# A LoRA-adapted linear layer on one core: four 8 MB chunks in three buffers in place of eight 4 MB chunks in six, and a small early store cut into seven

## The chip, the cores and the metric

The kernel runs on one core of a Trainium2 chip. Its engines work side by side and wait for each other by semaphores: TensorE (PE; PEld is its loading of weights) multiplies, VectorE (DVE), ScalarE (ACT) and GpSimd (POOL) copy and cast, and SyncE (SP) issues the transfers, which sixteen DMA engines carry out between the chip's main memory (DRAM) and the core's own memory (SBUF, 128 partitions). TensorE writes into PSUM. The metric is the device time of one execution in microseconds; less is better.

## The reference

```python
x_flat = x.reshape(-1, in_dim)            # x: 16 x 2048 x 256, float32
y = x_flat @ W                            # W: 256 x 256
lora_out = x_flat @ lora_A                # 256 x 16
lora_out = lora_out * lora_E
lora_out = lora_out @ lora_B              # 16 x 256
y = y + scale * lora_out
```

The 32,768 rows of x are 33.5 MB, and the output is as large. The rest is small.

## The kernel before

The low-rank part is folded into the weights once: W_eff = W + A (E scale B) is made at the start (lines 213 to 223 on TensorE, 165 to 177 on VectorE) and kept in bf16. After that each row of x is multiplied by a 256 x 256 matrix.

The rows are cut into eight chunks (`N_CHUNKS`) of 4 MB. In a chunk each partition holds 32 consecutive rows (`ROWS`) of 1 KB, so one transfer of a chunk is 128 contiguous pieces of 32 KB, one a partition. A chunk is loaded into a buffer of its own, a "home"; there are six (`N_HOMES`), 192 KB a partition. The result of a chunk is written over its input in the same home and stored from there. Chunks 6 and 7 use the homes of chunks 0 and 1 again, and their loads wait for the stores of those (line 105). The first chunk is loaded in three pieces of 8, 8 and 16 rows a partition, so that work can begin sooner (`LOAD_PIECES`).

Inside, the work goes by groups of four rows a partition (`CG`), 64 groups in all. Each group passes four engines:

- GpSimd casts 128 x 1024 float32 values to bf16 into `stage` (line 151). At a piece's first group it waits for that piece's load (line 148).
- TensorE transposes the group (line 196), two bf16 values at a time as one float32 word; ScalarE copies the result from PSUM to `xt` (line 162).
- TensorE multiplies (line 204, eight matmuls), and VectorE copies the product from PSUM back to the home (line 181). After a chunk's last group it signals `s_chunk`; after the very first group it signals `s_first`.

`stage`, `xt` and the two PSUM tiles are double-buffered.

All transfers are issued by SyncE, in the order of the list `ORDER`, into one queue. The DMA engines work that queue off in order: a transfer that is issued early stands behind those issued before it. A store (`S0` to `S7`) is issued when its chunk is done (line 127). All of a chunk must be done, as it is stored by one transfer. The last entry of `ORDER` is issued after the block of the five programs (line 241).

One transfer is unusual: after the loads of chunk `EARLY_AFTER`, SyncE waits for the first group (line 124) and stores 16 partitions x 128 bytes of the first result (line 125). The full store S0 writes the same bytes again later, after a wait for that early store (line 129).

Of the kernel before, what the change touches and what calls it, by code (L numbers as in the profile page):

```python
# [10 lines left out]
ALU = mybir.AluOpType  # L11


ROWS = 32
N_CHUNKS = 8
N_HOMES = 6
LOAD_PIECES = {0: [8, 8, 16]}

ORDER = [
    "L0", "L1", "L2", "L3", "L4", "L5",  # L20
    "S0", "S1", "L6", "L7", "S2", "S3", "S4", "S5", "S6", "S7",
]

EARLY_AFTER = 1

CG = 4
GPC = ROWS // CG
N_GROUPS = N_CHUNKS * GPC

# [6 lines left out]
def kernel(  # L36
# [16 lines left out]
    KT = K // P  # L53
    assert N == N_CHUNKS * ROWS * P and K == M and KT == 2

    x_chunks = x_flat.rearrange("(c p b) k -> c p b k", p=P, b=ROWS)
    y_chunks = out_flat.rearrange("(c p b) m -> c p b m", p=P, b=ROWS)

    sbuf, psum, sem = nc.alloc_sbuf_tensor, nc.alloc_psum_tensor, tc.alloc_semaphore
    homes = [sbuf(f"home{h}", [P, ROWS, K], FP32) for h in range(N_HOMES)]  # L60
    stage = [sbuf(f"stage{i}", [P, CG, K], BF16) for i in range(NS)]
# [12 lines left out]
    pieces = []  # L74
    for c in range(N_CHUNKS):
        s = 0
        for n in LOAD_PIECES.get(c, [ROWS]):
            pieces.append((c, s, s + n))
            s += n
    loaded = {pc: sem(f"loaded_{pc[0]}_{pc[1]}") for pc in pieces}  # L80
    set_up_loaded = {n: sem(f"loaded_{n}") for n in ("w", "a", "b", "e")}
    stored_of = {c: sem(f"stored_{c}") for c in range(N_CHUNKS - N_HOMES)}
    stored_rest = sem("stored_rest")
# [10 lines left out]
    s_early = sem("early_stored")  # L94

    def home(c):
        return homes[c % N_HOMES]

    sync, gpsimd, scalar, vector, tensor = nc.sync, nc.gpsimd, nc.scalar, nc.vector, nc.tensor

    def sync_program():
        def load(pc):
            c, s, e = pc
            if c >= N_HOMES:
                sync.wait_ge(stored_of[c - N_HOMES], 16)
            sync.dma_start(out=home(c)[:, s:e, :], in_=x_chunks[c, :, s:e, :]).then_inc(loaded[pc], 16)

        load(pieces[0])
        for name, to, of in (
            ("w", w_sb, W.rearrange("(q t) m -> q t m", t=KT)),  # L110
            ("a", a_sb, lora_A.rearrange("(q t) r -> q t r", t=KT)),
            ("e", e_sb, lora_E[:, None]),
            ("b", b_sb, lora_B),
        ):
            sync.dma_start(out=to[:], in_=of).then_inc(set_up_loaded[name], 16)
        for step in ORDER[:-1]:
            c = int(step[1:])
            if step[0] == "L":
                for pc in pieces:
                    if pc[0] == c and pc != pieces[0]:  # L120
                        load(pc)
                if c == EARLY_AFTER:

                    sync.wait_ge(s_first, 1)
                    sync.dma_start(out=y_chunks[0, :16, 0, :32], in_=home(0)[:16, 0, :32]).then_inc(s_early, 16)
            else:
                sync.wait_ge(s_chunk, c + 1)
                if c == 0:
                    sync.wait_ge(s_early, 16)
                sync.dma_start(out=y_chunks[c], in_=home(c)[:]).then_inc(stored_of.get(c, stored_rest), 16)  # L130

    def gpsimd_program():
# [97 lines left out]
    with tc.tile_critical(no_gpsimd_drain=True):  # L230
        sync_program()
        gpsimd_program()
        scalar_program()
        vector_program()
        tensor_program()
# [3 lines left out]

    last = int(ORDER[-1][1:])  # L240
    nc.sync.dma_start(out=y_chunks[last], in_=home(last)[:])
# [35 lines left out]
```

## Time and profile before

| What | Value |
|---|---|
| Time, median of 9 runs | 164.93 us (164.56 to 165.23) |
| Time of the profiled execution | 164.85 us |
| Its span, from the first to the last instruction | 163.1 us (163.07) |
| Mean granted TensorE clock | 0.828 |
| Bytes moved, mean rate | 67.43 MB, 414 GB/s |
| TensorE matmuls busy | 99.6 us (61%) |
| VectorE busy, copies of line 181 | 79.5 us (49%), 64 of 1225 ns |
| GpSimd busy, casts of line 151 | 67.1 us (41%), 64 of 1040 ns |
| ScalarE busy, copies of line 162 | 66.1 us (41%), 64 of 1012 ns |
| Issue to landing of a 4 MB load, median | 20.0 us |
| Issue to landing of a 4 MB store, median | 42.0 us |

The last two rows contain the time that a transfer stands in the queue. In the slice rows of the page the span is cut into 40 equal parts, and each digit is a busy share in tenths (9 is 90% or more); PEclk is the TensorE clock that was granted. The view of one DMA queue gives its packets, their MB, and the time that they took as a share of sixteen engines' time; small packets of 4 bytes are the semaphore writes that end each transfer on each engine.

### The profile page before, as it was taken

To read this page: it belongs to the slowest core of one execution; us is meant where nothing else is said; L and a number is where in the kernel's file an instruction comes from. 1 tells how busy PE (TensorE), PEld (TensorE's weight loads), DVE (VectorE), ACT (ScalarE), POOL (GpSimd) and SP (SyncE) were. 2 spreads that over 40 slices of the span, in tenths; PEclk is the share of its full clock that TensorE was granted. 3 is DMA by queue.
4 is the path that set the end of the run, shared out by engine and by line. 5 is a ranking of instruction groups with operands and counts; after the bars stand their busy time and mean duration, and the time that the engine had idled before them with its cause. 6 is when DMAs were issued, how large, how long until landed. Compare 5 with 4: busy or idle time off the path is not lost. (4 is left out here: it accounts for less than half of the span.)

```text
span 163.1 us, 2148 instructions
## 1 busy us (share of the span) xinstructions
PE 99.6 (61%) x778; PEld 82.4 (51%) x778; DVE 79.5 (49%) x66; ACT 66.1 (41%) x65; POOL 67.1 (41%) x70
## 2 busy tenths in 40 slices
PE   0399948999999999999930099999960000000000
PEld 0268837888888888888820078888840000000000
DVE  0115862788888888888860025888880000000000
ACT  3043732777767676777720025677720000000000
POOL 1444615777777777777500155777500000000000
PEclk9999995999999999999996557999997555555555
DMA  4999998998998999899999999999999999999990
GB/s 163 420 450 454 394 507 386 434 466 386 490 410 386 506 394 388 386 434 460 402 434 450 410 466 410 420 458 410 418 466 410 450 434 418 466 402 426 458 402 16
DMA packets 2979, 67.43 MB, mean 414 GB/s; under 512 B 528, under 2 KB 544, under 8 KB 672
## 3 DMA queue, kind: packets, MB, share of 16 engines
q1 hardware_dynamic: 2976, 67.41, 96.9%
q14 instruction: 3, 0.02, 0.0%
HBM read 33.85 MB, written 33.56 MB: 413 GB/s over the span
## 5 line engine op out<-in xcount | busy, mean ns | idle before, releaser
L181 DVE COPY home<-psum_y 128x1024 f32<-128x1024 f32 x64 | 78.4, 1225 | 32.8 <-PE psum_y L204 29.9
L151 POOL CAST stage<-home 128x1024 bf16<-128x1024 f32 x64 | 66.4, 1040 | 48.8 <-PE psum_xt L196 24.9
L162 ACT COPY xt<-psum_xt 128x1024 bf16<-128x1024 bf16 x64 | 64.8, 1012 | 52.7 <-PE psum_xt L196 52.7
L204 PE MATMUL psum_y<-weff,xt 128*128 128x256 bf16 x512 | 70.3, 283 | 0.7
L204 PEld LDWEIGHTS psum_y<-weff,xt 128*128 128x128 bf16 x512 | 48.2, 101 | 14.9 <-issue 6.7
L196 PE MATMUL psum_xt<-ident,stage 128*128 128x128 f32 x260 | 42.6, 291 | 14.0 <-PEq L189 14.0
L196 PEld LDWEIGHTS psum_xt<-ident,stage 128*128 128x128 f32 x260 | 33.1, 151 | 16.1 <-issue 15.1
L216 PE MATMUL psum_y<-ident,a_sb 128*16 128x128 f32 x2 | 0.6, 397 | 6.7 <-DMA a_sb<-in_lora_A_dram 6.7
L167 DVE TENSOR_SCALAR ate<-psum_y,e_sb 16x256 f32<-16x256 f32 x1 | 0.5, 472 | 7.4 <-PE psum_y L216 7.4
L216 PEld LDWEIGHTS psum_y<-ident,a_sb 128*16 128x16 f32 x2 | 0.1, 88 | 6.7 <-issue 6.7
L222 PE MATMUL psum_y<-b_sb,ate 16*128 16x256 f32 x4 | 2.1, 670 | 0.0
L177 DVE TENSOR_TENSOR weff<-w_sb,psum_y 128x512 bf16<-128x512 f32 x1 | 0.7, 687 | 2.4 <-PE psum_y L222 2.4
L162 ACT ACT_TABLE_LOAD x1 | 1.3, 1283 | 0.9 <-SPq L230 0.9
L222 PEld LDWEIGHTS psum_y<-b_sb,ate 16*128 16x128 f32 x4 | 1.2, 320 | 0.5 <-issue 0.3
L133 POOL MEMSET ident<- 128x128 f32 x1 | 0.2, 204 | 0.5 <-SPq L230 0.5
L135 POOL TENSOR_SCALAR_AFFINE_SELECT ident<-ident 128x128 f32<-128x128 f32 x1 | 0.3, 292 | 0.2 <-POOL ident L133 0.2
L258 POOL MEMSET const-float32-0.0<- 128x1 f32 x1 | 0.1, 98 | 0.2 <-issue 0.2
L258 POOL MEMSET const-bfloat16-1.0<- 128x1 bf16 x1 | 0.1, 102 | 0.0
L258 POOL MEMSET const-uint8-127<- 128x1 uint8 x1 | 0.1, 102 | 0.0
L258 POOL MEMSET const-float32-1.0<- 128x1 f32 x1 | 0.1, 98 | 0.0
## 6 DMA issues: line engine op xcount, KB each, us to landing
out_dram<-home SPq DMA_DIRECT2D x8, 4096.0 KB, 42.0
home<-in_x_dram SPq DMA_DIRECT2D x7, 4096.0 KB, 20.0
home<-in_x_dram SPq DMA_DIRECT2D x2, 1024.0 KB, 5.2
home<-in_x_dram SPq DMA_DIRECT2D x1, 2048.0 KB, 10.1
w_sb<-in_W_dram SPq DMA_DIRECT2D x1, 256.0 KB, 5.0
a_sb<-in_lora_A_dram SPq DMA_DIRECT2D x1, 16.0 KB, 4.7
e_sb<-in_lora_E_dram SPq DMA_DIRECT2D x1, 0.1 KB, 4.5
b_sb<-in_lora_B_dram SPq DMA_DIRECT2D x1, 16.0 KB, 4.0
```

Of the source, the lines that this page charges most:

```text
L133: gpsimd.memset(ident[:], 0.0).then_inc(s_ident, 1)
L135: gpsimd.affine_select(out=ident[:], in_=ident[:], compare_op=ALU.not_equal, fill=1.0, base=0, pattern=[[-1, P]], channel_multiplier=1,).t ...
L151: gpsimd.tensor_copy(out=stage[g % NS][:], in_=home(c)[:, b:b + CG, :]).then_inc(s_stage, 1)
L162: scalar.copy(out=xt[g % NX][:], in_=halves).then_inc(s_xt, 1)
L167: vector.tensor_scalar(out=ate[:], in0=psum_y[0][:R, :KT, :P], scalar1=e_sb[:], scalar2=float(scale), op0=ALU.mult, op1=ALU.mult,).then_in ...
L177: vector.tensor_add(out=weff[:], in0=w_sb[:], in1=psum_y[1][:, :KT, :]).then_inc(s_free, NY)
L181: vector.tensor_copy(out=home(c)[:, b:b + CG, :], in_=psum_y[g % NY][:]).then_inc(s_free, 1)
L196: ins = tensor.transpose(psum_xt[i % NT][:, b, :], words[:, b, :], ident[:])
L204: ins = tensor.matmul(psum_y[i % NY][:, b, :], xt[i % NX][:, b, t, :], weff[:, t, :], start=(t == 0), stop=(t == KT - 1),)
L216: ins = tensor.transpose(psum_y[0][:R, t, :P], a_sb[:, t, :], ident[:])
L222: ins = tensor.matmul(psum_y[1][:, t, :], ate[:, t, :], b_sb[:], start=True, stop=True)
L258: nc = _bacc.Bacc("TRN2", target_bir_lowering=False, num_devices=1)
```

## The change

Eight chunks of 32 rows a partition become four of 64. A home is twice as large, and three take the place of six, so the memory used is the same. A chunk's transfer is 128 pieces of 64 KB. Chunk 0 is loaded in four pieces (8, 8, 16 and 32 rows), chunk 3 in two of 32; chunks 1 and 2 in one. The order keeps its kind: loads into all homes, two stores, the load that reuses a home, the remaining stores.

The early store is issued after the load of chunk 0 rather than of chunk 1 (in both cases 8 MB of loads stand ahead of it), and is seven transfers in place of one. They store 8, 4, 12, 14, 15, 2 and 1 partitions, 128 bytes each, from different places of the first group's four rows. S0 waits for all of them.

```diff
-ROWS = 32
-N_CHUNKS = 8
-N_HOMES = 6
-LOAD_PIECES = {0: [8, 8, 16]}
-
-ORDER = [
-    "L0", "L1", "L2", "L3", "L4", "L5",
-    "S0", "S1", "L6", "L7", "S2", "S3", "S4", "S5", "S6", "S7",
-]
-
-EARLY_AFTER = 1
+ROWS = 64
+N_CHUNKS = 4
+N_HOMES = 3
+LOAD_PIECES = {0: [8, 8, 16, 32], 3: [32, 32]}
+
+ORDER = ["L0", "L1", "L2", "S0", "S1", "L3", "S2", "S3"]
+
+EARLY_AFTER = 0
+EARLY_LINES = [8, 4, 12, 14, 15, 2, 1]
...
                     sync.wait_ge(s_first, 1)
-                    sync.dma_start(out=y_chunks[0, :16, 0, :32], in_=home(0)[:16, 0, :32]).then_inc(s_early, 16)
+                    for b, n in enumerate(EARLY_LINES):
+                        sync.dma_start(out=y_chunks[0, :n, b % CG, b // CG * 32:][:, :32], in_=home(0)[:n, b % CG, b // CG * 32:][:, :32]).then_inc(s_early, 16)
...
                 if c == 0:
-                    sync.wait_ge(s_early, 16)
+                    sync.wait_ge(s_early, 16 * len(EARLY_LINES))
```

## The prediction

> **What bounds the kernel now.** I read the page's DMA rows first. 67.4 MB go through one DMA queue, and the sixteen DMA engines are full from the first slice to the last but one; TensorE has gaps, and its clock falls in two of them.
>
> ```profile
> PEclk9999995999999999999996557999997555555555
> DMA  4999998998998999899999999999999999999990
> q1 hardware_dynamic: 2976, 67.41, 96.9%
> ```
>
> Next I read the DMA view of 124 to 158 us, where nothing computes and only stores run, and of 8.2 to 13 us, where 128 packets of 16 KB run.
>
> ```profile
> DMA packets 499, 14.78 MB, mean 435 GB/s; under 512 B 48, under 2 KB 48, under 8 KB 48
> q1 hardware_dynamic: 499, 14.78, 100.6%
> ...
> DMA packets 143, 2.09 MB, mean 435 GB/s; under 512 B 15, under 2 KB 15, under 8 KB 15
> q1 hardware_dynamic: 143, 2.09, 101.9%
> ```
>
> A packet is one partition's contiguous piece. In the first view 451 are of 32 KB: 1.006 x 16 x 34 us / 451 = 1.213 us each; in the second 1.019 x 16 x 4.8 / 128 = 0.611 us. The individual packet records give 1,209.5 and 607.4 ns from one start to the next on an engine, so 2 x 607.4 - 1209.5 = 5 ns of a packet are fixed and the rest is bytes. One 4 MB chunk is 8 packets an engine, 9.68 us with its completion. I call this a unit. The order before is 6 units of loads, 2 of stores (S0, S1), 2 of loads (L6, L7), 6 of stores.
>
> The tail shows that the engines don't end together. This is the DMA view of 158 to 163.1 us, 40 slices of 0.13 us:
>
> ```profile
> GB/s 0 771 1285 257 257 257 0 0 0 257 0 0 0 0 0 0 0 0 257 0 0 0 0 0 0 0 0 0 0 0 0 0 0 0 0 0 0 0 0 0
> ```
>
> Fifteen engines have started their last packet by 158.7 and end by 159.9; one starts packets at 159.2 and 160.4 and ends at 161.62. The span ends 1.45 us after that. By the packet records one engine takes 1,284 to 1,293 ns a packet from 63.5 to 82.7 and one again from 105 to 122.7, some 77 ns too many, while the others take 1,213. Those are the stores S0, S1 and S2, S3, during which compute runs; beside L6 and L7, and in S4 to S7 where compute has ended, none is slow. I read it as one engine that is slow where stores and compute overlap; that is inferred from four stretches.
>
> Last I read the timeline for compute, which is hidden under DMA and must only be early enough. These are GpSimd's first and last cast of the last two chunks, VectorE's last copies, and SyncE's issue of the last store (start, us, engine).
>
> ```profile
> 92.99 2.02 POOL L151 CAST stage<-home 128x1024 bf16<-128x1024 f32 x2 [12.69 <-DMA home<-in_x_dram]
> ...
> 115.81 1.04 POOL L151 CAST stage<-home 128x1024 bf16<-128x1024 f32 x1 [0.31 <-PE psum_xt L196]
> ...
> 119.62 2.58 DVE L181 COPY home<-psum_y 128x1024 f32<-128x1024 f32 x2 [0.24 <-PE psum_y L204]
> 122.59 0.33 SPq L241 DMA_DIRECT2D out_dram<-home  x1
> ```
>
> Sixteen groups (64 rows) take 122.20 - 92.99 = 29.2 us from the first cast, 0.53 us after L6's last packet ended at 92.46. S7, issued at 122.59, first moves bytes at 149.3: 27 us of slack.
>
> **The change, part by part.** *Descriptors.* Of L1, L2 and S0 to S3, 48 packets of 64 KB an engine replace 96 of 32 KB: 48 x 5 ns = 0.24 us less. Six completions fewer at 6 ns add 0.04. No row has a 64 KB packet or a 64 KB step between partitions. Nearest are 16 KB and 32 KB packets, both at 27 GB/s an engine, so by these 0.28 us is gained; if each is cut into two again, nothing. I take 0.2.
>
> *Early store.* Each 128-byte packet with its completion takes 22 ns in the records. If a DMA puts one line on an engine, the most is 7 x 22 = 0.15 us; all 56 lines on one engine would be 1.2; an engine with none saves 0.02. I take 0.1. The Trainium skill (DMA: Bandwidth & Descriptors, "Why a DMA increments its semaphore by 16 and not by 1") says that a DMA uses the largest number of engines up to 16 that divides its slowest dimensions, the lowest-numbered ones. By that engine 0 would get seven packets, engine 15 none, which makes the estimate a staircase of 0 to 0.15 us; the trace has 16 lines only, so no row shows it.
>
> On SyncE the wait for the first group's copy (to 14.34) now stands before L1 and L2. The same 8 MB are queued ahead, which last to 22.8, and seven issues at 0.35 to 0.47 us put L1 at 17.0 to 17.6. A load's first packet follows its issue by 1.0 to 1.45 us (0.94 to 1.96 and 2.40 in the opening), so 3.7 us of cover remain and this costs nothing. The wait ahead of S0 has until 62 us.
>
> *Coarser chunks in the middle.* Chunk 0 ends where chunk 1 did, at 40.6; the first 64-row load lands at 42.65 (unit 4) instead of 32-row ones at 32.9 and 42.65. TensorE waits some 3 us; with 29.2 us for the chunk it ends by 72.4, and S1 is needed at 81.5: 7.7 us of cover after issue and latency. Chunk 2 landed at 62.7 and ends at most 16 x 1.41 = 22.6 later, 95; S2's place in the queue comes at 120. L3 waits for S0, about 83, and is needed at 101. These cost nothing while the covers last. Where loads first give way to stores the DMA view of 59 to 62.5 us has 367 GB/s, some 0.5 us lost; the change keeps that place, and so, I take it, that loss.
>
> *The end, where the cover goes.* L3 is units 11 and 12, S2 units 13 and 14, S3 units 15 and 16. Before, the last loads were units 9 and 10 and six stores stood behind them. Now the last 64 rows must be computed between the landing of L3's first half and the end of S2, three units or 29 us, and S3 can't start on any row before all are done. Worked out:
>
> - L7 ended on its last engine at 102.53. Less 0.2 and plus 0.1 from above. The slow engine now also meets compute in the first half of S1 (to about 93, not 82.7): 8 packets x 77 ns = 0.6 more, bounds -1.1 (no lag at all) to 0.7. One more load unit, 9.68: L3's first half ends at 112.7, the first cast is at 113.2.
> - Sixteen groups: 29.2 from the row above; the second half is there at 122.9, before group 9 (11.5 us after the first cast) needs it, so they run through. The restart after 93 us is cold, as it was before.
>
> ```profile
> 25.03:28.45 3.42, 3.42 (x17) 2.81 (x17) 0.82 (x1) 1.01 (x1) 1.75 (x2) 0.50 1.07 460
> 86.47:100.12 13.65, 5.95 (x28) 4.97 (x29) 1.78 (x2) 2.02 (x2) 4.10 (x4) 0.50 1.01 435
> ```
>
> (Stretch, its length, busy time of PE, PEld, DVE, ACT and POOL, granted clock, DMA share, GB/s.) TensorE restarted at 24.90 and was at full clock at 28.45, 3.5 us; at 94.17 and full at 100.12, 5.95 us. Cold groups take 2.5 us, warm ones 1.41, so a cold stretch as short as the first saves 2.4 x (1 - 1.41/2.5) = 1.1 us. I take 28.9, with 28.1 to 29.2. The Trainium skill (TensorE: Matmul & The Clock Gate, "What's actually happening") has the window of 3.4 us run free of the kernel; by it the cold time could be 3.4 to 6.8 us and differ between runs, which would stretch my upper end by 0.4.
>
> - Last copy ends at 142.1; issue 0.39 later as before (122.20 to 122.59); first packet 1.0 to 1.45 later, I take 1.2: 143.7. S2 would have ended at 139.4 on the fifteen engines and near 143 on the slow one, so the queue is empty for up to 4 us.
> - S3's eight packets of 64 KB an engine are 8 x 2.414 = 19.3; first packets from a standing queue took 0.2 to 0.7 us too long in the opening (8 KB ones), I take 0.3, with 0 to 0.7: end 163.3, tail 1.45, span 164.75.
>
> Against its own span of 163.07 that is +1.7. The profiled execution took 164.85 us, 0.08 under the median, so the time is 164.93 + 1.7 = 166.6 us. The lag of the one engine is absorbed in the wait; only 0.3 us would have been gained had the queue stayed full.
>
> **Rivals.** *Last chunk late* (forecast, 166.6, own range 165.3 to 167.8): for it speaks that three units are 29.0 us and cast, compute, issue and latency are 0.53 + 28.9 + 0.39 + 1.2 = 31.0. Against it: by the slow engine, whose S2 takes 16 x 77 ns = 1.2 us longer, only 0.8 of the 2.0 is idle.
>
> *Faster, the lag goes.* If the uneven early lines or longer packets keep the slow engine from falling behind, L3's first half lands by 111.0, cast 111.5; with the short cold stretch 28.1, issue 0.39, latency 1.0 and no slow first packet, S3 starts at 141.0 and ends at 160.3: span 161.8, time 163.6. It decides from about 2 us off my sum, and needs both the lag and the cold time to shrink; the packet rows show the lag unchanged by an early store of one packet an engine.
>
> *No change.* Lag as before and the short cold stretch: the sum falls by 0.6 + 0.8 to 165.2, and with the short latency of 1.0 us to 165.0.
>
> *Slower by rate.* 64 KB pieces or pitch move fewer bytes: 48 x 2.41 = 116 us are exposed, 1% is 1.2 us, 167.8 with the gap. Against it: 16 and 32 KB run at one rate. *It doesn't do what it says*: packets stay at 32 KB; 166.8, as the gap comes from the order.
>
> **How the numbers follow.** About 0.2% is what a measurement of this kernel can tell from no change. Last chunk late 0.71 (packets cut again within it), rate 0.09, no change 0.07, lag gone 0.13. Slower: 0.80; same 0.07; faster 0.13. Range 164.8 to 167.8: it takes in the bounds of lag, cold time and latency, and leaves most of the faster case and the rate case out.
>
> **What would show it.** A gap of 1 to 4 us in the DMA slices near 140 to 144; the last issue of SyncE at about 142.5 rather than 122.6; GpSimd's wait for the last load ended at 113.2 (111.5 would be the lag gone); engines ending together instead of 2.6 us apart; 64 KB packets at 2.41 us. If the DMA row has no gap before the last store, the forecast is wrong in its main step.

## The result and the profile after

The changed kernel is slower: 165.45 us (median of 19 runs, 165.06 to 166.02) against 164.78 us for the kernel before in runs beside it (57 runs, 164.41 to 165.3). The ratio is 1.0042, with a 95% interval of 1.0034 to 1.0051, or +0.7 us where +1.7 was forecast. The profiled execution took 165.57 us, its span is 163.79 us; before it was 163.07. The time lies inside the range and on the side that was forecast; the difference came out 1 us smaller.

The same rows of the page, now of the changed kernel:

```profile
PEclk9999985799879999999999965555599999955555
DMA  5999999979969989699799899989999989659955
q1 hardware_dynamic: 2192, 67.41, 96.4%
```

Over the span the DMA engines are nearly as full as before (96.4% against 96.9%); the slices of 6 and 5 from 139.2 us on hold a gap. SyncE's issues from 70 us on (start, us, engine):

```profile
71.21 0.34 SPq L129 DMA_DIRECT2D out_dram<-home  x1
83.50 1.02 SPq L104 DMA_DIRECT2D home<-in_x_dram  x2
118.38 0.34 SPq L129 DMA_DIRECT2D out_dram<-home  x1
142.11 0.34 SPq L240 DMA_DIRECT2D out_dram<-home  x1
```

These are S1, L3's two halves, S2 and S3. The last store is issued at 142.11, near the forecast of 142.5, and by then the queue has run dry. The DMA view of 136 to 150 us in 40 slices of 0.35 us shows it:

```profile
DMA  0009994000040000000990000099000009900000
GB/s 0 0 0 562 1123 1123 187 0 0 0 0 187 0 0 0 0 0 0 0 1311 1685 0 0 0 0 0 1311 1685 0 0 0 0 0 1872 1123 0 0 0 0 0
```

The packets are in step, and their starts stand in bunches; the row counts a packet's bytes where it starts. By the packet records, fifteen engines started their last packet of S2 by 138.2 and ended between 139.60 and 140.6; one started its last at 140.16 and ended at 142.65. All sixteen start S3 at 142.95 to 143.10. So fifteen engines wait for 2.4 to 3.35 us, and one for 0.3. They also end together, within 0.15 us, where one engine trailed before. Here are 158 to 163.79 us in slices of 0.14 us:

```profile
GB/s 0 0 0 0 0 0 0 0 0 0 0 0 0 5886 1358 0 0 0 0 0 0 0 0 0 0 0 0 0 0 0 0 0 0 0 0 0 0 0 0 0
```

The compute between L3's first half and S3: GpSimd's first cast of the chunk and VectorE's last two copies.

```profile
113.06 2.02 POOL L150 CAST stage<-home 128x1024 bf16<-128x1024 f32 x2 [24.75 <-DMA home<-in_x_dram]
...
139.13 2.58 DVE L180 COPY home<-psum_y 128x1024 f32<-128x1024 f32 x2 [0.24 <-PE psum_y L203]
```

Sixteen groups take 139.13 + 2.58 - 113.06 = 28.65 us. TensorE's clock was low from 95.16 to 119.05 (the first two numbers are the stretch and its length, the 0.50 is the granted clock):

```profile
95.16:119.05 23.89, 4.80 (x23) 3.92 (x24) 1.22 (x1) 2.02 (x2) 4.10 (x4) 0.50 0.97 418
```

### The profile page after: what moved, and what is told of

Same layout as the page of the kernel before. It is cut to its first block, busy times and chain, and to the rows that moved or that the text cites. A ratio compares the mean times of both kernels' runs of the same rounds, so it can differ in the third digit from the quotient of the medians.

```text
span 163.8 us, 2142 instructions
## 1 busy us (share of the span) xinstructions
PE 100.7 (61%) x778; PEld 83.4 (51%) x778; DVE 79.5 (49%) x66; ACT 66.1 (40%) x65; POOL 67.0 (41%) x70
## 3 DMA queue, kind: packets, MB, share of 16 engines
q1 hardware_dynamic: 2192, 67.41, 96.4%
## 5 line engine op out<-in xcount | busy, mean ns | idle before, releaser
L180 DVE COPY home<-psum_y 128x1024 f32<-128x1024 f32 x64 | 78.4, 1224 | 52.4 <-PE psum_y L203 49.9
L203 PE MATMUL psum_y<-weff,xt 128*128 128x256 bf16 x512 | 71.2, 285 | 0.9
L203 PEld LDWEIGHTS psum_y<-weff,xt 128*128 128x128 bf16 x512 | 48.7, 102 | 15.1 <-issue 7.0
L195 PEld LDWEIGHTS psum_xt<-ident,stage 128*128 128x128 f32 x260 | 33.6, 153 | 34.6 <-issue 33.6
```

What stands on the lines that cost most here:

```text
L180: vector.tensor_copy(out=home(c)[:, b:b + CG, :], in_=psum_y[g % NY][:]).then_inc(s_free, 1)
L195: ins = tensor.transpose(psum_xt[i % NT][:, b, :], words[:, b, :], ident[:])
L203: ins = tensor.matmul(psum_y[i % NY][:, b, :], xt[i % NX][:, b, t, :], weff[:, t, :], start=(t == 0), stop=(t == KT - 1),)
```

## The experiments

Times are medians; each ratio is to the kernel before in runs on the same chip, with its 95% interval.

**E1, the last store in two halves.** It takes away what makes S3 wait for all 64 rows.

```diff
+            if g == N_GROUPS - GPC // 2 - 1:
+                vector.drain().then_inc(s_half, 1)
...
+                if step == ORDER[-1]:
+                    sync.wait_ge(s_half, 1)
+                    sync.dma_start(out=y_chunks[c, :, :32, :], in_=home(c)[:, :32, :]).then_inc(stored_rest, 16)
...
-    nc.sync.dma_start(out=y_chunks[last], in_=home(last)[:])
+    nc.sync.dma_start(out=y_chunks[last, :, 32:, :], in_=home(last)[:, 32:, :])
```

> The changed kernel with its last store in two halves; the first half (32 rows a partition) is issued as soon as its eight groups are done. Theory A (the queue runs empty before the last store, and behind that gap the one engine that is slow beside compute sets the next limit): no gap; that engine ends S2 at 142.65 and needs 16 packets of 1.21 us more, so it ends at 162.0 and the span is 163.3 to 163.5 (163.8 in the changed kernel), the time 165.0 to 165.2; the engines end some 3 us apart again. Theory B (the loss comes from larger packets or the seven early stores, not from the gap): the time stays at 165.4 to 165.5. Theory C (the gap is all of it, no engine lags behind it): the time falls to 164.5 or lower, as the packets alone save 0.2 to 0.3.

165.25 us, ratio 1.0025 (1.0013 to 1.0037). The half stores are issued at 130.88 and 142.50:

```profile
118.46 0.34 SPq L134 DMA_DIRECT2D out_dram<-home  x1
130.88 0.34 SPq L129 DMA_DIRECT2D out_dram<-home  x1
142.50 0.33 SPq L247 DMA_DIRECT2D out_dram<-home  x1
```

The gap is gone, and one engine trails again, which I call the trailing engine from here on. Its tail, 158 to 163.5 us in slices of 0.14 us:

```profile
GB/s 477 238 715 1907 238 0 238 0 0 0 0 0 238 0 0 0 0 0 0 0 0 238 0 0 0 0 0 0 0 0 0 0 0 0 0 0 0 0 0 0
```

Fifteen engines end between 159.25 and 160.1 and one at 162.14 (expected 162.0). Theory A holds for where the end comes from. By the medians and ratios the gap cost 0.2 to 0.3 us, not 0.7: without it the kernel is still 0.48 us slower than before. The size is rough: the intervals of the two ratios overlap, and the fastest run of the changed kernel (165.06) equals the fastest of E1 (165.07).

**E6, the same gap closed in another way**: `LOAD_PIECES` for chunk 3 is [8, 8, 16, 32] instead of [32, 32].

> The changed kernel with the load of the last chunk in pieces of 8, 8, 16 and 32 rows, so that its groups begin some 7 us earlier. Theory A: the groups of the last 32 rows start at 122.8 with TensorE warm, the last store is issued near 139.5, before the lagging engine is free; that engine (S2 to 142.7, then 19.3) sets the end, span 163.3 to 163.6, time 165.1 to 165.3, as with the store in two halves. If the lag did not matter: 164.5.

165.13 us, ratio 1.0020 (1.0010 to 1.0030). The last store is issued 2 us earlier:

```profile
140.09 0.34 SPq L240 DMA_DIRECT2D out_dram<-home  x1
```

Most engines still wait some 0.8 us or less for it, but the trailing engine goes from S2 to S3 without a wait and ends at 162.00, within 0.15 us of its end in E1.

**E5, the suspected cost enlarged**: L3 in one piece.

> The changed kernel with the load of the last chunk in one piece, so that its work begins a half chunk later (the suspected cost, enlarged). Theory A: the load lands at 122.2, first cast 122.8, 28.65 us of groups to 151.4, issue 151.8, first packet 152.7, store 19.5, tail 1.3: span 173.5, time 175.2. Theory B: within 0.5 us of 165.45.

175.29 us in one run, span 173.50; 175.2 and 173.5 were expected. The last store is issued at the time that the sum gives, which supports the chain from the load's landing over sixteen groups to the store:

```profile
128.21 0.33 SPq L129 DMA_DIRECT2D out_dram<-home  x1
151.80 0.33 SPq L240 DMA_DIRECT2D out_dram<-home  x1
```

**E2, TensorE kept warm.** 22 passes of eight matmuls before the transposes of chunk 3.

```diff
...
+        for i in range(UNROLL):
+            if i == UNROLL - 1:
+                with tensor.Fori(0, WARM):
+                    for t in range(8):
+                        tensor.matmul(psum_z[:], weff[:, 0, :P], weff[:, t % KT, :], start=True, stop=True)
+            turn(i + 1)
+            multiply(i)
...
```

> The changed kernel with 176 matmuls more on TensorE, into a PSUM tile that nobody reads, between chunk 2 and chunk 3, so that its clock is full when chunk 3 lands. Theory A: the 16 groups of chunk 3 take 27.2 to 27.6 us instead of 28.65, the last store is issued near 140.9 instead of 142.1, the lagging engine (S2 until 142.65) then sets the end: span 163.3 to 163.5, time 165.0 to 165.2, and the runs lie closer together than the 165.06 to 166.02 of the changed kernel. Theory B: 165.4 to 165.5 as before. If TensorE's own work is what slows the one DMA engine beside stores, that engine is slow to the end of S1 (102) instead of 93 and L3 lands 0.5 us later, which would eat half of the gain.

166.3 us in six runs from 165.59 to 166.69, ratio 1.0091 (1.0064 to 1.0118): a miss. The profiled run, 165.59, is the fastest of the six, so the trace doesn't show where the others lost their time; that stays open. It does show two things. The matmuls ended too early (at 111.2), the clock fell again at 114.7, and it was full at 118.08; with this shorter cold stretch the sixteen groups took 28.15 us. And TensorE alone keeps one DMA engine slow. In this window of 92 to 102 us nothing else computes but VectorE's last copy at its start (busy us of PE, PEld, DVE, ACT and POOL):

```profile
92.00:102.00 10.00, 10.00 (x94) 8.96 (x93) 1.22 (x1) 0.02 (x1) 0.00 (x0) 1.00 0.91 389
```

The records of S1 have one engine at 2,535 to 2,581 ns a 64 KB packet up to 103.26, where the others take 2,418; in the changed kernel the last such packet ends at 90.6, as TensorE stops (90.9). L3 was there 0.46 us later than in the changed kernel (first casts at 113.52 and 113.06).

The executions with the same sixteen groups give the price of the cold clock (at half speed, 0.50 in the rows above):

| Kernel | TensorE restart | full clock | cold us | groups us |
|---|---|---|---|---|
| before | 94.17 | 100.12 | 5.95 | 29.21 |
| E1 | 114.33 | 119.78 | 5.45 | 28.97 |
| after | 114.25 | 119.05 | 4.80 | 28.65 |
| E5 | 124.08 | 128.58 | 4.50 | 28.50 |
| E3 | 114.45 | 118.00 | 3.54 | 28.22 |
| E2 | 114.70 | 118.08 | 3.38 | 28.15 |

From last to first, (29.21 - 28.15) / (5.95 - 3.38) = 0.41 us a cold us. The low stretches shown here and in the prediction last 3.42, 13.65 and 23.89 us, which are 1, 4 and 7 times 3.41. The Trainium skill (TensorE: Matmul & The Clock Gate, "What's actually happening") speaks of a free-running window of 3.4 us; cold stretches of 3.38 to 5.95 us with one and the same restart agree with it.

**E3, one early store of 16 lines** (`EARLY_LINES = [16]`), **and E4, the seven early stores in the kernel before.**

> The changed kernel with one early store of 16 lines in place of seven. Theory A: the early stores only shift engines by at most 0.15 us ahead of loads that are never short: 165.35 to 165.55, no difference. Theory B: the staircase matters; the time moves by more than 0.2 us (down if it costs, up if it spreads the engines usefully).

> The kernel before with the seven early stores in place of one. Theory A: no difference, 164.7 to 164.9. Theory B: more than 0.2 us either way.

E3: 165.51 us, 1.0051 (1.0036 to 1.0067). E4: 164.85 us, 1.0008 (0.9996 to 1.0020). The seven early stores are no part of the difference that can be measured: in neither kernel does their number move the time beyond the intervals.

**E7, what slows the one engine.** The kernel before, with work of one engine after the other beside S4 to S7, and a staircase of early stores: 1 to 15 lines of 4 KB, which S0 stores again.

```diff
+STAIR = list(range(1, 16))
...
+                    for n in STAIR:
+                        sync.dma_start(out=y_chunks[0, at:at + n, :CG, :], in_=home(0)[at:at + n, :CG, :]).then_inc(s_early, 16)
+                        at += n
...
+        for _ in range(32):
+            ins = tensor.matmul(psum_z[:], weff[:, 0, :P], weff[:].rearrange("p t m -> p (t m)"), start=True, stop=True)
...
+        for _ in range(70):
+            ins = tensor.matmul(psum_z[:, :64], weff[:, 0, :P], weff[:, 0, :64], start=True, stop=True)
```

> The kernel before with two additions. (1) A staircase of early stores, 4 KB a line over 1 to 15 lines, which sets the DMA engines 0.15 us apart from one another, so that each can be followed in the packet records. (2) After the last group, while S4 to S7 run alone, work that touches no result: 32 matmuls of 512 columns, then 70 matmuls of 64 columns, 7 copies on ScalarE, 110 copies of 8 columns on VectorE, 70 one-column memsets on GpSimd, one engine after the other, about 7 us each. Theory A1 (TensorE's work slows one DMA engine beside stores): 32 KB packets of 1.27 to 1.30 us on one engine in the two matmul stretches, and 1.213 in the other three. Theory A2 (any engine's instructions do it, by their number): slow packets also beside the small copies and memsets, and fewer beside the 32 long matmuls. Theory A3 (compute has nothing to do with it): no slow packets after 124 us.

167.93 us in one run, with more bytes and more work than the kernel before. The five pieces of work in the timeline (start, us):

```profile
123.95 7.08 PE L252 MATMUL psum_z<-weff 128*128 128x512 bf16 x32 [1.37 <-DVEq L202]
130.87 2.21 PE L255 MATMUL psum_z<-weff 128*128 128x64 bf16 x70
133.11 7.50 ACT L177 COPY xt<-stage 128x1024 bf16<-128x1024 bf16 x7 [11.85 <-PE psum_z L255]
140.68 8.16 DVE L205 CAST xt<-ident 128x8 bf16<-128x8 f32 x110 [16.83 <-ACTq L179]
148.91 2.38 POOL L165 MEMSET stage<- 128x1 bf16 x70 [30.40 <-DVE xt L205]
```

The packets of 32 KB beside each on the engine that is hit, from the packet records; the other engines take 1,213 ns, but for one packet of 1,613 at 129.39 that starts as a load of 16 KB of instructions ends:

```
beside                          instructions per us    packet, ns       extra ns per instruction
32 long matmuls + weight loads  64 / 7.1 = 9.0         1,236 to 1,241   25 / (9.0 x 1.24) = 2.2
70 short ones + weight loads    140 in 2.4             1,340, 1,434     348 / 140 = 2.5
7 copies on ScalarE             0.9                    1,216 to 1,218   3 to 5 ns a packet
110 small copies on VectorE     110 / 8.2 = 13.5       1,242 to 1,265   38 / (13.5 x 1.25) = 2.3
70 small memsets on GpSimd      70 in 2.4              1,312, 1,284     170 / 70 = 2.4
```

Theory A2 holds: it is the number of instructions, some 2.3 ns each, whichever engine runs them and however much they compute. In the kernel a group of 27 instructions takes 1.41 us, so a slow packet of 1.29 us meets some 25 of them, 57 ns at 2.3 each; 61 to 89 ns were measured, mostly 71 to 80. The other 20 ns or so aren't assigned to anything here. The engine that is hit also followed the staircase: 9 or 10 of the fifteen early lines lie on it, so it isn't the one with the most or the fewest. What it has to do for each instruction isn't shown. Every run of this case was profiled, so none can tell whether the profile's own records are what it carries.

**E8 and E9, fewer instructions in both kernels.** Six of eight matmuls of a group are left out from the fifth group on, so most of the output isn't computed.

```diff
-        def multiply(i):
+        def multiply(i, lines=CG):
...
-            for b in range(CG):
+            for b in range(lines):
...
-        with tensor.Fori(0, N_GROUPS // UNROLL):
+        for i in range(UNROLL):
+            turn(i + 1)
+            multiply(i)
+        with tensor.Fori(0, N_GROUPS // UNROLL - 1):
             for i in range(UNROLL):
                 turn(i + 1)
-                multiply(i)
+                multiply(i, 1)
```

> The kernel before with two matmuls instead of eight in every group after the fourth (three of four rows are not multiplied, their output is left over). A group then has 15 instead of 27 instructions, and nothing of the transfers changes. Theory A2 (each instruction beside a store costs one DMA engine some 2.3 to 3 ns, and that engine ends the kernel): its slow packets shrink from +77 ns to +35 to 50, its lag at the end from 2.6 to about 1.3 us, and the time falls by 0.9 to 1.3 us to 163.5 to 163.9, though compute was never the bound. Theory A3 (the lag doesn't come from instructions, or doesn't set the end): 164.6 to 164.9.

> The changed kernel with the same matmuls left out. Compute of the last chunk shrinks to some 25 us (VectorE then bounds a group at 1.25 us), so the last store is issued near 138.6, before S2 ends on the lagging engine, and the lag is small: both costs of the change are taken away together. Theory A: what remains is the gain of the packets, 0.2 to 0.3 us, less a remaining gap of up to 0.3: the time lies 0.0 to 0.3 us below the other kernel of this pair. Theory B (larger packets or early stores cost): it stays 0.5 or more above it.

E8: 163.91 us, ratio 0.9957 (0.9939 to 0.9975), 0.86 below the kernel before, just short of what was expected. The span fell by more, from 163.07 to 161.81: outside the span E8 and E9 each take some 2.1 us where the other kernels take 1.8. The slow packets mostly take 1,255 to 1,279 ns (more than the 1,248 to 1,263 expected), and the last engine trails by 1.3 us instead of 2.6. Its tail, 158 to 161.8 us in slices of 0.1 us, has no starts after 159.15:

```profile
GB/s 345 0 345 1725 345 345 0 345 0 0 0 690 0 0 0 0 0 0 0 0 0 0 0 0 0 0 0 0 0 0 0 0 0 0 0 0 0 0 0 0
```

So the trailing engine does set the end of the kernel before, though compute is never its bound.

E9: 164.36 us, 0.9974 (0.9963 to 0.9986), and 0.45 us above E8 where 0 to 0.3 below was expected: a miss that told most. There is no gap, as S2 ends from 140.04 on and the last store is issued well before:

```profile
136.63 0.34 SPq L243 DMA_DIRECT2D out_dram<-home  x1
```

Still the larger packets lose. Even the first engine to end does so at 159.36, 0.32 later than in E8 (159.04). (E9's profiled run, 164.93, is the slowest of its twelve; E8's, 163.89, lies at its median.)

**Where the larger packets lose.** Laid side by side, the packet records of all kernels differ most where loads first give way to stores: at the end of L5 before S0 in the kernel before, at the end of L2 before S0 in the changed one. Here is the DMA view of 59 to 63 us, first of the kernel before:

```profile
q1 hardware_dynamic: 64, 1.57, 108.3%
```

then of the changed kernel:

```profile
q1 hardware_dynamic: 48, 2.10, 146.4%
```

Counted by their starts: before, 1.57 MB are 48 packets of 32 KB, which took 1.083 x 64 / 48 = 1.444 us each, 0.231 too long; three an engine make 0.69 us lost. After, 2.10 MB are 32 packets of 64 KB at 1.464 x 64 / 32 = 2.93 us each instead of 2.418; two an engine make 1.0 us lost. It is the last load packets that are slow, not the stores: each engine's semaphore write for the load follows them (62.16 to 62.75 before, 62.28 to 62.95 after), and the store packets behind it take 1,213 and 2,418 ns. Before, the last two packets of L5 on each engine share the loss; after, the last one of L2 has all of it, 3,047 to 3,764 ns. From here on this is called the loss at the first stores. The records of the whole transition give 0.61 to 0.74 us in three kernels with 32 KB packets (before, E4, E8) and 1.01 to 1.34 us in the seven with 64 KB (after, E1, E2, E3, E5, E6, E9). In E7, whose staircase had set the engines up to 2.5 us apart, it was 0.16 us. E9 loses 1.22 us and E8 0.74 in this way, and the difference of 0.48 is about what E9 is slower (0.45). That was no test yet: it sets single profiles side by side, and in E7 bytes and order differ too.

**E10 to E12, engines set apart.** A staircase of early stores that S0 doesn't store again, so that no bytes are added: 2 KB and 1 KB lines in the kernel before, 4 KB lines in the changed one.

```diff
...
+                    for n in STAIR:
+                        sync.dma_start(out=y_chunks[0, at:at + n, :SR, :], in_=home(0)[at:at + n, :SR, :]).then_inc(s_early, 16)
+                        at += n
...
+                    sync.dma_start(out=y_chunks[0, at:, :SR, :], in_=home(0)[at:, :SR, :]).then_inc(stored_of[0], 16)
+                    sync.dma_start(out=y_chunks[0, :, SR:, :], in_=home(0)[:, SR:, :]).then_inc(stored_of[0], 16)
```

> The changed kernel with early stores of 4 KB a line over 1 to 15 lines, not stored again by S0, in place of its seven: the bytes stay the same, but the engines stand up to 2.5 us apart, a 64 KB packet's time. Theory D (where loads first give way to stores the engines lose time because they switch together, and more with long packets: 0.67 us an engine before, 1.0 to 1.3 in all kernels with 64 KB, 0.17 in the probe whose engines stood apart): the loss there falls below 0.5 us, L3's first half lands some 0.5 us earlier, the time falls to 164.7 to 165.2. If the loss belongs to the first stores as such: 1.0 us stays, and 165.3 to 165.8.

> The kernel before with early stores of 2 KB a line over 1 to 15 lines, not stored again by S0; engines up to 1.3 us apart, a 32 KB packet's time. Theory D: the loss at the first stores falls from 0.67 to 0.2 to 0.4 us; the engine that ends last bears about 0.2 us more bytes than the mean, so the time falls by 0.1 to 0.4 to 164.35 to 164.65. If the loss belongs to the first stores as such: 164.8 to 165.0.

> The same with 1 KB a line: engines up to 0.7 us apart. Theory D: the loss lies between, 0.4 to 0.6 us, and the time at 164.5 to 164.75. If the loss belongs to the first stores as such: 164.75 to 164.95.

The loss went where the theory said for two of three: 0.02 us in E12 (from 1.0), 0.20 in E10, but 0.76 in E11, unchanged. The same window in E12, 24 packets at 0.906 x 64 / 24 = 2.42 us:

```profile
q1 hardware_dynamic: 25, 1.57, 90.6%
```

The times went the other way: E12 166.15 us, 1.0069 (1.0051 to 1.0088); E10 165.26, 1.0020 (1.0010 to 1.0030); E11 165.52, 1.0040 (1.0026 to 1.0055). Each is above even what was expected if the loss stayed. What the transition gives back the spread seems to take: a load has landed only when its last engine is done. In E12 L3's first half ended at 113.34 on that engine, 0.8 later than in the changed kernel, and in E10 the last engine trails the first by 3.1 us at the end instead of 2.6. So no run shows that a kernel gets faster when this loss is taken away; that it makes the changed kernel slower is argued from E8, E9 and the records. No complete version here beats the kernel before; E8 and E9 are faster only because they leave work out.

## Why the prediction was right or wrong

**Right: place and order of the chain.** Each step is there in the trace, in the order of the sum. What failed is the size of its terms, the closing ones above all: all but one came out smaller than forecast.

| Term | forecast | measured |
|---|---|---|
| first cast of chunk 3 | 113.2 | 113.06 |
| sixteen groups | 28.9 | 28.65 |
| last copy to issue | 0.39 | 0.40 |
| issue to first packet | 1.2 | 0.84 |
| S3, first to last packet | 19.3 + 0.3 | 19.55 |
| tail | 1.45 | 1.29 |
| span | 164.75 | 163.79 |

The largest error is "first packet 1.0 to 1.45 later, I take 1.2", where 0.84 was measured, under its lower bound. The term came from the kernel's opening, where five transfers start at once from nothing. A store into an empty queue took 0.82 to 0.85 us in all six kernels where one occurs (after, E2, E3, E5, E6, E12). Next is the cold clock: 28.9 for 28.65, inside its bounds, with 4.80 us cold. The tail was read where one engine ended alone; when all end together it is 1.29 to 1.36. A difference of 1.7 us was made of two ends of 163 us, and 1 us of small errors on one side took more than half of it. That the first cast is only 0.14 us off is in part luck. The loss before the first stores, put at no change, grew by some 0.33 us. Against that, L7's last packet before, from 100.96 to 102.54 on the trailing engine, was 0.36 us too long; the sum starts from its end, and the changed kernel has no such packet ahead of that cast.

**Wrong: what the gap is worth.** "The lag of the one engine is absorbed in the wait; only 0.3 us would have been gained had the queue stayed full." Half of it is true: the engines end together. What failed is the count of what a full queue would give. With the queue full for the engine that ends last (E1, E6) the kernel is 0.3 to 0.5 us slower than before, not 0.3 faster. The gap is some 0.3 us of the 0.67. For the rest the records show two parts, which no run takes apart. The trailing engine meets more stores beside compute: 27 slow packets of 32 KB before, 2.05 us too long in all, and 18 of 64 KB in E1, 2.65 us. The prediction counted part of this for the landing, but it should have been counted for the end of the kernel too: the engine trails by 2.9 us in E1 against 2.64 before. And the loss at the first stores grew.

**Wrong: "the change keeps that place, and so, I take it, that loss".** It kept the place, and the loss went from 0.67 to 1.0 to 1.3 us, by more than the packets save. The saving itself is there: 2,414 ns from start to start for 64 KB against 2 x 1,209.5, the 5 ns that were forecast, 0.24 us in all.

**Wrong, without effect: the cover of S2.** Chunk 2 was to be done by 95 at most. S2 was issued at 118.38, since TensorE's order turns the next group (line 196 before) ahead of multiplying the last one, so that a chunk's last group waits for the next chunk's load. Its place in the queue came at 120.28: less than 2 us of cover where 25 were counted. In the kernel before, S5 stood behind L6 in the same way (issued at 98.30), and had time.

**Right:** the early stores cost nothing that can be measured (E3, E4), and no cover in the middle ran out. **The rivals:** rate did not fall (2,418 ns a packet); packets stayed at 64 KB; the lag did not go. One part of "slower by rate" was real, at one place and for 1 us.

The rule on the early stores that stood in the prediction (the Trainium skill, DMA: Bandwidth & Descriptors, "Why a DMA increments its semaphore by 16 and not by 1") agrees with what is seen: 56 packets of 128 bytes come unevenly, none on the engine that starts L1 last (the records don't number the engines), and in E7 the fifteen steps of 0.16 us leave the engines 2.5 us apart.

## What to carry to other kernels

When transfers are made coarser, work out the last one first: how much must be computed between the last landing and the end of the queue ahead of the last store, and which single DMA engine gets there last. A gap on fifteen engines costs only what the sixteenth doesn't hide, so find what that one would do with the gap closed before pricing the gap. The Trainium skill (Perfetto Trace Analysis, "DMA Optimizations") advises larger transfers, with 2 KB made 4 or 8 KB as its example. Here, from 32 to 64 KB, 5 ns were left to win on a packet, while the last loads ahead of the first stores lost 0.3 to 0.7 us more than before.

## What the hardware did unexpectedly

- One DMA engine is slower while it stores beside running instructions, by about 2.3 ns for each instruction of any engine (E7), and not while it loads (1,213 to 1,224 ns for every 32 KB load packet that starts from 27 to 58 us, beside compute, in the kernel before). It set the end of the kernel before: with fewer instructions the time fell by 0.86 us (E8).
- Where loads first give way to stores in one queue, engines in step lose 0.61 to 0.74 us each on the last load packets of 32 KB and 1.0 to 1.3 us with 64 KB, 0.76 when they stand up to 0.7 us apart (E11), and 0.02 to 0.2 us when they stand 1.3 us or more apart (E7, E10, E12). Later changes from loads to stores cost 0.06 us or less, on the mean of the engines, in the kernels before, after, E1 and E8. Why the first differs stays open.
- In E11 two engines lost 1.03 and 1.08 us on one packet there. One of the packets starts as a load of 8 KB of instructions ends (60.91 to 61.22 us); in the changed kernel the packet behind such a load (122.94 to 123.25) is 0.41 us too long. For the rest the trace shows no cause.
